# Average pooling over a 537 MB tensor: two loads of a partition from one run of 128 KB, their means in one store run of 32 KB

## The chip, the core and the metric

The kernel runs on one core of a Trainium2 chip. A core has an on-chip memory (SBUF) of 128 partitions, 16 DMA engines that move data between SBUF and the chip's main memory (HBM), and engines with a program each. Three of them matter here: VectorE (DVE) adds, ScalarE (ACT) scales and issues most stores, SyncE (SP) issues the loads. What SP issues goes through one queue (q1 in the profile) and what ACT issues through another (q10); both queues are worked off by the same 16 DMA engines. The metric is the time of one execution on the device in microseconds; less is better.

## The reference

```python
def setup_inputs():
    return {"x": np.random.randn(64, 256, 8192).astype(np.float32),
            "kernel_size": 4, "stride": 4}

def reference(x, kernel_size, stride):
    batch, channels, length = x.shape
    out_len = (length - kernel_size) // stride + 1
    output = np.zeros((batch, channels, out_len), dtype=np.float32)
    for i in range(out_len):
        start = i * stride
        output[:, :, i] = np.mean(x[:, :, start : start + kernel_size], axis=2)
    return output
```

Every four neighbouring numbers of the last axis become their mean. Window and step are equal and divide the row, so the whole tensor can be taken as one flat line of 134,217,728 numbers in groups of four: 536.87 MB are read and 134.22 MB are written, whatever the tiling.

## The kernel before

The flat line is cut into 64 **blocks** of 8.39 MB. A block lies in HBM as 128 rows of 64 KB (`FULL` = 16384 numbers), one row to each partition, one behind the other: partition p of block n has the row n·128 + p. Two input buffers (`xt0`, `xt1`, 64 KB in each partition) hold one block each, even blocks in the first and odd ones in the second. Two output buffers (`ot0`, `ot1`, 32 KB in each partition) hold the means of a **pair** of blocks each, 16 KB for a block.

A block goes through four steps. SP loads it (`load`, line 62, a DMA of 128 rows of 64 KB). DVE adds neighbours in place (line 75, 16384 numbers of a partition become 8192) and adds neighbours again into the output buffer (line 77, 4096 sums). When both blocks of a pair are summed, ACT multiplies the whole output buffer by 1/4 (line 93). Then ACT issues one store of the pair (line 96): 2 × 128 rows of 16 KB, since in HBM the means of one block form a stretch of 2 MB and those of the next block the stretch after it.

```python
xb = x.rearrange("b c l -> (b c l)").rearrange("(n p m) -> n p m", p=P, m=FULL)
ob = out.rearrange("b c l -> (b c l)").rearrange("(n p m) -> p n m", p=P, m=M)
```

The order is written out by hand, with semaphores. `take(engine, sem, n)` (line 59) lets an engine wait until a semaphore has reached n, and takes n off it. DVE waits for `full[k]` (the load of buffer k has landed) and, at the first block of a pair, for `stored[q]` (the store that last read the output buffer has landed). After the second addition DVE raises `free`; SP waits for it and issues the load of the block after the next into the buffer just freed. So while DVE works on one buffer, the load of the other one is in the queue or on its way. ACT waits for `summed`, and its store for the end of its own multiplication (`scaled`).

The loop (line 115) does four blocks a turn, 60 in all. The last four are written out. Blocks 60 and 61 (lines 122 to 139): each is scaled by itself, the first is stored by ACT (line 135), the second by SP (line 139), where its store stands in SP's queue behind the loads of blocks 62 and 63. Block 62 (lines 141 to 148) is scaled by itself and stored by SP. Block 63 comes in two loads of 128 rows of 32 KB (`TAIL`, line 112); each half is summed, scaled (line 156) and stored by ACT (line 158, 128 rows of 8 KB). Last, SP waits for all stores.

Of the kernel before, what the change touches and what calls it, by code (L numbers as in the profile page):

```python
# [1 line left out]

# [4 lines left out]


FULL = 16384
PAIR = 2  # L10
ROUND = 2 * PAIR

TAIL = (8192, 8192)


@with_exitstack
def kernel(
    ctx: ExitStack,
    tc: tile.TileContext,
    x: bass.AP,  # L20
    kernel_size: bass.AP,
    stride: bass.AP,
    out: bass.AP,
):
    nc = tc.nc
    K, S = int(kernel_size), int(stride)
    assert K == S == 4
    B, C, L = x.shape
    assert L % K == 0
    P = nc.NUM_PARTITIONS  # L30
    dt = x.dtype
    add, mult = mybir.AluOpType.add, mybir.AluOpType.mult

    M = FULL // K
    blocks = B * C * L // P // FULL
    loop = blocks - ROUND
    assert blocks * P * FULL == B * C * L and blocks % ROUND == 0 and sum(TAIL) == FULL
    xb = x.rearrange("b c l -> (b c l)").rearrange("(n p m) -> n p m", p=P, m=FULL)
    ob = out.rearrange("b c l -> (b c l)").rearrange("(n p m) -> p n m", p=P, m=M)


    xt0 = ctx.enter_context(nc.sbuf_tensor([P, FULL], dt))
    xt1 = ctx.enter_context(nc.sbuf_tensor([P, FULL], dt))
    ot0 = ctx.enter_context(nc.sbuf_tensor([P, PAIR * M], dt))
    ot1 = ctx.enter_context(nc.sbuf_tensor([P, PAIR * M], dt))
    xt, ot = [xt0, xt1], [ot0, ot1]


    full = [nc.alloc_semaphore(f"full{k}") for k in range(2)]
    piece = [nc.alloc_semaphore(f"piece{k}") for k in range(len(TAIL))]  # L50
    free = nc.alloc_semaphore("free")
    summed = nc.alloc_semaphore("summed")
    summed_last = nc.alloc_semaphore("summed_last")
    scaled = nc.alloc_semaphore("scaled")
    scaled_last = nc.alloc_semaphore("scaled_last")
    stored = [nc.alloc_semaphore(f"stored{k}") for k in range(2)]

    def take(engine, sem, n):
        engine.wait_ge(sem, n).then_inc(sem, -n)  # L59

    def load(i, k):
        d = nc.sync.dma_start(out=xt[k][:, :], in_=xb[i])
        d.then_inc(full[k], 16)
        return d

    for k in range(2):
        tc.no_tile_sem_insts.add(load(k, k).ins.name)
    tc.close()  # L70
    tc.compile()  # L71

    def sums(t, o):
        w = t.shape[1]
        nc.vector.tensor_tensor(out=t[:, : w // 2], in0=t[:, ::2], in1=t[:, 1::2], op=add)  # L75
        nc.vector.drain()
        return nc.vector.tensor_tensor(  # L77
            out=o, in0=t[:, : w // 2 : 2], in1=t[:, 1 : w // 2 : 2], op=add
        )

    def pair(i, q, ahead):

        for k in range(PAIR):
            take(nc.vector, full[k], 16)
            if k == 0:
                take(nc.vector, stored[q], 16)
            sums(xt[k][:, :], ot[q][:, k * M : (k + 1) * M]).then_inc(free, 1)
            take(nc.sync, free, 1)
            if k == 1:
                nc.sync.sem_inc(summed, 1)  # L90
            ahead(k)
        take(nc.scalar, summed, 1)
        nc.scalar.mul(ot[q][:, :], ot[q][:, :], 1.0 / K).then_inc(scaled, 1)  # L93
        take(nc.scalar, scaled, 1)
        o = ot[q][:, :].rearrange("p (n m) -> p n m", n=PAIR)
        nc.scalar.dma_start(out=ob[:, bass.ds(i, PAIR), :], in_=o).then_inc(stored[q], 16)


    zero = nc.const_aps.tensor(0.0, [P, 1], dt)
    nc.scalar.mul(ot[0][:, :1], zero, 1.0).then_inc(stored[0], 16)  # L100
    nc.scalar.sem_inc(stored[1], 16)

    edges = [sum(TAIL[:i]) for i in range(len(TAIL) + 1)]
    pieces = list(zip(edges[:-1], edges[1:]))
    xe, oe = xb[blocks - 1], ob[:, blocks - 1, :]

    def ahead_of_last(k):
        if k == 0:
            load(blocks - 2, 0)
        else:  # L110
            for sem, (a, b) in zip(piece, pieces):
                nc.sync.dma_start(out=xt[1][:, a:b], in_=xe[:, a:b]).then_inc(sem, 16)

    engines = (mybir.EngineType.SP, mybir.EngineType.DVE, mybir.EngineType.Activation)
    with nc.Fori(0, loop // ROUND, 1, engines=engines) as r:
        for q in range(2):
            i = r * ROUND + q * PAIR
            pair(i, q, lambda k: load(i + (PAIR + k), k))

    for k in range(PAIR):
        o = ot[0][:, k * M : (k + 1) * M]
        take(nc.vector, full[k], 16)
        if k == 0:
            take(nc.vector, stored[0], 16)
        sums(xt[k][:, :], o).then_inc(free, 1)
        take(nc.sync, free, 1)
        nc.sync.sem_inc(summed, 1)
        ahead_of_last(k)  # L130
        take(nc.scalar, summed, 1)
        if k == 0:
            nc.scalar.mul(o, o, 1.0 / K).then_inc(scaled, 1)  # L133
            take(nc.scalar, scaled, 1)
            nc.scalar.dma_start(out=ob[:, loop, :], in_=o).then_inc(stored[0], 16)
        else:
            nc.scalar.mul(o, o, 1.0 / K).then_inc(scaled_last, 1)  # L137
            take(nc.sync, scaled_last, 1)
            nc.sync.dma_start(out=ob[:, loop + 1, :], in_=o).then_inc(stored[0], 16)

    take(nc.vector, stored[1], 16)
    take(nc.vector, full[0], 16)
    o = ot[1][:, :M]
    sums(xt[0][:, :], o).then_inc(summed_last, 1)
    take(nc.scalar, summed_last, 1)
    nc.scalar.mul(o, o, 1.0 / K).then_inc(scaled_last, 1)  # L146
    take(nc.sync, scaled_last, 1)
    nc.sync.dma_start(out=ob[:, blocks - 2, :], in_=o).then_inc(stored[1], 16)


    for sem, (a, b) in zip(piece, pieces):
        o = ot[1][:, M + a // K : M + b // K]
        take(nc.vector, sem, 16)
        sums(xt[1][:, a:b], o).then_inc(summed_last, 1)
        take(nc.scalar, summed_last, 1)
        nc.scalar.mul(o, o, 1.0 / K).then_inc(scaled, 1)  # L156
        take(nc.scalar, scaled, 1)
        nc.scalar.dma_start(out=oe[:, a // K : b // K], in_=o).then_inc(stored[1], 16)
    take(nc.sync, stored[0], 32)
    take(nc.sync, stored[1], 16 * (1 + len(TAIL)))  # L160


# [1 line left out]
_INS = ['x', 'kernel_size', 'stride']  # L164
_OUTS = [((64, 256, 2048), 'float32')]

_NUMBERS = {'kernel_size': 4, 'stride': 4}


# [26 lines left out]
```

## Time and profile before

| what | value |
|---|---|
| median of 3 runs | 1553.11 us (1552.67 to 1555.31) |
| profiled execution, its own time | 1553.16 us |
| span of the profiled execution | 1551.8 us |
| DVE busy | 839.9 us (54%) |
| ACT busy | 227.0 us (15%) |
| 16 DMA engines, moved over the span | 671.10 MB, 432 GB/s |
| DMA packets, both queues | 18240 |

The span runs from the first to the last record of the execution; the own time is 1.36 us longer. "Busy" of an engine counts its instructions, not its waiting and not its issuing of DMAs. A DMA engine works its queue off in packets; here a packet is one row of a transfer (64, 32, 16 or 8 KB) or the 4 bytes that raise the semaphore when the engine's share is done. A transfer of 128 rows gives each of the 16 engines 8 rows and one such mark. The trace has a record of each packet, with its start, its duration and its queue; the 18240 packets are 8064 rows of 64 KB, 256 of 32 KB, 8064 of 16 KB, 256 of 8 KB, and 1600 marks.

### The profile page before, as it was taken

Reading aid. Unit: us, or ns where it says so; the run is one execution under the profiler, and the core shown is the slowest. Engines: PE = TensorE matmul, PEld = TensorE weight load, DVE = VectorE, ACT = ScalarE, POOL = GpSimd, SP = SyncE. Lnnn points to the kernel's source line nnn. Section 1 sums busy time; section 2 is a strip of 40 time slices with the busy share of each in tenths; the row PEclk is TensorE's granted clock in tenths of the full one; section 3 lists DMA queues with packets and bytes.
Section 4 is the critical chain, followed back from the end, with each engine's and each line's share of the span. In section 5 each row is a group of like instructions: output and inputs, shape, how many; then the busy total and the mean of one; then the engine's idle time right before and its main releaser. Section 6 shows DMA issues by size and latency. Waiting matters only on the chain. (4 is left out here: it accounts for less than half of the span.)

```text
span 1551.8 us, 942 instructions
## 1 busy us (share of the span) xinstructions
DVE 839.9 (54%) x130; ACT 227.0 (15%) x37; POOL 0.2 (0%) x4
## 2 busy tenths in 40 slices
DVE  3645646456465564654646546455464554645546
ACT  0111011110111101111011110111101111011111
POOL 0000000000000000000000000000000000000000
DMA  9999999999999999999999999999999999999999
GB/s 414 419 444 441 417 439 432 439 441 416 433 432 439 446 434 417 432 433 446 439 436 434 413 440 439 439 432 438 414 439 439 432 439 438 416 437 432 439 432 413
DMA packets 18240, 671.10 MB, mean 432 GB/s; under 512 B 1600, under 2 KB 1600, under 8 KB 1600
## 3 DMA queue, kind: packets, MB, share of 16 engines
q1 hardware_dynamic: 9648, 541.07, 80.5%
q10 hardware_dynamic: 8592, 130.03, 19.6%
HBM read 536.87 MB, written 134.22 MB: 432 GB/s over the span
## 5 line engine op out<-in xcount | busy, mean ns | idle before, releaser
L75 DVE TENSOR_TENSOR xt<-xt 128x8192 f32<-128x8192 f32 (+1 forms) x65 | 556.5, 8561 | 699.4 <-DVEq L59 699.4
L93 ACT ACTIVATE ot<-ot 128x8192 f32<-128x8192 f32 x30 | 210.9, 7029 | 1246.2 <-ACTq L59 1246.2
L77 DVE TENSOR_TENSOR ot<-xt 128x4096 f32<-128x4096 f32 (+1 forms) x65 | 283.4, 4360 | 4.9
L146 ACT ACTIVATE ot<-ot 128x4096 f32<-128x4096 f32 x1 | 3.6, 3616 | 20.6 <-ACTq L59 20.6
L137 ACT ACTIVATE ot<-ot 128x4096 f32<-128x4096 f32 x1 | 3.6, 3616 | 20.3 <-ACTq L59 20.3
L133 ACT ACTIVATE ot<-ot 128x4096 f32<-128x4096 f32 x1 | 3.6, 3616 | 17.4 <-ACTq L59 17.4
L156 ACT ACTIVATE ot<-ot 128x2048 f32<-128x2048 f32 x2 | 3.8, 1909 | 12.1 <-ACTq L59 12.1
L100 ACT ACT_TABLE_LOAD x1 | 1.3, 1283 | 2.4 <-PEq L71 2.4
L100 ACT ACTIVATE ot<-const-float32-0.0 128x1 f32<-128x1 f32 x1 | 0.2, 202 | 0.0
L177 POOL MEMSET const-bfloat16-1.0<- 128x1 bf16 x1 | 0.1, 102 | 0.0
L177 POOL MEMSET const-uint8-127<- 128x1 uint8 x1 | 0.1, 102 | 0.0
L177 POOL MEMSET const-float32-0.0<- 128x1 f32 x1 | 0.1, 99 | 0.2 <-issue 0.2
L177 POOL MEMSET const-float32-1.0<- 128x1 f32 x1 | 0.1, 99 | 0.0
## 6 DMA issues: line engine op xcount, KB each, us to landing
out_dram<-ot ACTq DMA_DIRECT2D x30, 4096.0 KB, 51.7
xt<-in_x_dram SPq DMA_DIRECT2D x2, 4096.0 KB, 29.9
out_dram<-ot SPq DMA_DIRECT2D x2, 2048.0 KB, 27.2
out_dram<-ot ACTq DMA_DIRECT2D x1, 2048.0 KB, 45.3
out_dram<-ot ACTq DMA_DIRECT2D x2, 1024.0 KB, 9.1
xt<-in_x_dram SPq DMA_DIRECT2D x63, 34.7
```

The source lines that it names most:

```text
L75: nc.vector.tensor_tensor(out=t[:, : w // 2], in0=t[:, ::2], in1=t[:, 1::2], op=add)
L77: return nc.vector.tensor_tensor(out=o, in0=t[:, : w // 2 : 2], in1=t[:, 1 : w // 2 : 2], op=add)
L93: nc.scalar.mul(ot[q][:, :], ot[q][:, :], 1.0 / K).then_inc(scaled, 1)
L100: nc.scalar.mul(ot[0][:, :1], zero, 1.0).then_inc(stored[0], 16)
L133: nc.scalar.mul(o, o, 1.0 / K).then_inc(scaled, 1)
L137: nc.scalar.mul(o, o, 1.0 / K).then_inc(scaled_last, 1)
L146: nc.scalar.mul(o, o, 1.0 / K).then_inc(scaled_last, 1)
L156: nc.scalar.mul(o, o, 1.0 / K).then_inc(scaled, 1)
L177: nc = _bacc.Bacc("TRN2", target_bir_lowering=False, num_devices=1)
```

## The change

Blocks are paired in HBM too. A pair now is a **run** of 16.8 MB that lies in HBM as 128 rows of 128 KB, one for each partition. The first load of a run brings the first 64 KB of every such row, the second load the other 64 KB (`xr[n, k]`). So the rows of one load, still 64 KB long, are 128 KB apart instead of 64 KB. The means of a run are 32 KB in a row for each partition (`orun[n]`), and a store of a run is 128 rows of 32 KB. The 32 runs are numbered 0 to 31.

At the end, run 30 (blocks 60 and 61 before) goes through the same function `pair` as the loop's runs: scaled at once by ACT, and stored by SP in one store, which stands in SP's queue behind the loads of run 31. Run 31 has no store of its own for its first block: ACT scales the first block when the first half of the second is summed, scales that half, and stores both together (128 rows of 24 KB); the last half is stored as before (128 rows of 8 KB).

```diff
-    loop = blocks - ROUND
+    runs = blocks // PAIR
-    xb = x.rearrange("b c l -> (b c l)").rearrange("(n p m) -> n p m", p=P, m=FULL)
-    ob = out.rearrange("b c l -> (b c l)").rearrange("(n p m) -> p n m", p=P, m=M)
+    xr = x.rearrange("b c l -> (b c l)").rearrange("(n p k m) -> n k p m", p=P, k=PAIR, m=FULL)
+    orun = out.rearrange("b c l -> (b c l)").rearrange("(n p m) -> n p m", p=P, m=PAIR * M)
...
-    def load(i, k):
-        d = nc.sync.dma_start(out=xt[k][:, :], in_=xb[i])
+    def load(n, k):
+        d = nc.sync.dma_start(out=xt[k][:, :], in_=xr[n, k])
...
-    def pair(i, q, ahead):
+    def pair(n, q, ahead, store):
...
+        done = scaled if store is nc.scalar else scaled_last
         take(nc.scalar, summed, 1)
-        nc.scalar.mul(ot[q][:, :], ot[q][:, :], 1.0 / K).then_inc(scaled, 1)
-        take(nc.scalar, scaled, 1)
-        o = ot[q][:, :].rearrange("p (n m) -> p n m", n=PAIR)
-        nc.scalar.dma_start(out=ob[:, bass.ds(i, PAIR), :], in_=o).then_inc(stored[q], 16)
+        nc.scalar.mul(ot[q][:, :], ot[q][:, :], 1.0 / K).then_inc(done, 1)
+        take(store, done, 1)
+        store.dma_start(out=orun[n], in_=ot[q][:, :]).then_inc(stored[q], 16)
...
-    xe, oe = xb[blocks - 1], ob[:, blocks - 1, :]
+    xe, oe = xr[runs - 1, 1], orun[runs - 1]
...
-            load(blocks - 2, 0)
+            load(runs - 1, 0)
...
-    with nc.Fori(0, loop // ROUND, 1, engines=engines) as r:
+    with nc.Fori(0, (runs - 2) // 2, 1, engines=engines) as r:
         for q in range(2):
-            i = r * ROUND + q * PAIR
-            pair(i, q, lambda k: load(i + (PAIR + k), k))
+            n = r * 2 + q
+            pair(n, q, lambda k: load(n + 1, k), nc.scalar)
+    pair(runs - 2, 0, ahead_of_last, nc.sync)
-    for k in range(PAIR):
-        o = ot[0][:, k * M : (k + 1) * M]
...
-        if k == 0:
-            nc.scalar.mul(o, o, 1.0 / K).then_inc(scaled, 1)
-            take(nc.scalar, scaled, 1)
-            nc.scalar.dma_start(out=ob[:, loop, :], in_=o).then_inc(stored[0], 16)
-        else:
-            nc.scalar.mul(o, o, 1.0 / K).then_inc(scaled_last, 1)
-            take(nc.sync, scaled_last, 1)
-            nc.sync.dma_start(out=ob[:, loop + 1, :], in_=o).then_inc(stored[0], 16)
     take(nc.vector, stored[1], 16)
     take(nc.vector, full[0], 16)
-    o = ot[1][:, :M]
-    sums(xt[0][:, :], o).then_inc(summed_last, 1)
-    take(nc.scalar, summed_last, 1)
-    nc.scalar.mul(o, o, 1.0 / K).then_inc(scaled_last, 1)
-    take(nc.sync, scaled_last, 1)
-    nc.sync.dma_start(out=ob[:, blocks - 2, :], in_=o).then_inc(stored[1], 16)
-    for sem, (a, b) in zip(piece, pieces):
+    sums(xt[0][:, :], ot[1][:, :M]).then_inc(summed_last, 1)
+    for k, (sem, (a, b)) in enumerate(zip(piece, pieces)):
+        take(nc.vector, sem, 16)
+        sums(xt[1][:, a:b], ot[1][:, M + a // K : M + b // K]).then_inc(summed_last, 1)
+        if k == 0:
+            take(nc.scalar, summed_last, 1)
+            nc.scalar.mul(ot[1][:, :M], ot[1][:, :M], 1.0 / K)
         o = ot[1][:, M + a // K : M + b // K]
-        take(nc.vector, sem, 16)
-        sums(xt[1][:, a:b], o).then_inc(summed_last, 1)
         take(nc.scalar, summed_last, 1)
         nc.scalar.mul(o, o, 1.0 / K).then_inc(scaled, 1)
         take(nc.scalar, scaled, 1)
-        nc.scalar.dma_start(out=oe[:, a // K : b // K], in_=o).then_inc(stored[1], 16)
-    take(nc.sync, stored[0], 32)
-    take(nc.sync, stored[1], 16 * (1 + len(TAIL)))
+        c = 0 if k == 0 else M + a // K
+        d = M + b // K
+        nc.scalar.dma_start(out=oe[:, c:d], in_=ot[1][:, c:d]).then_inc(stored[1], 16)
+    take(nc.sync, stored[0], 16)
+    take(nc.sync, stored[1], 16 * len(TAIL))
```

More of the change, by code (lines that the diff above doesn't have):

```diff
@@ L68 @@
     for k in range(2):
-        tc.no_tile_sem_insts.add(load(k, k).ins.name)
+        tc.no_tile_sem_insts.add(load(0, k).ins.name)
     tc.close()
@@ L114 @@
     engines = (mybir.EngineType.SP, mybir.EngineType.DVE, mybir.EngineType.Activation)
-    with nc.Fori(0, loop // ROUND, 1, engines=engines) as r:
+    with nc.Fori(0, (runs - 2) // 2, 1, engines=engines) as r:
         for q in range(2):
-            i = r * ROUND + q * PAIR
-            pair(i, q, lambda k: load(i + (PAIR + k), k))
-    for k in range(PAIR):
-        o = ot[0][:, k * M : (k + 1) * M]
-        take(nc.vector, full[k], 16)
-        if k == 0:
[L126 to L132, printed above, removed]
-            nc.scalar.mul(o, o, 1.0 / K).then_inc(scaled, 1)
-            take(nc.scalar, scaled, 1)
-            nc.scalar.dma_start(out=ob[:, loop, :], in_=o).then_inc(stored[0], 16)
-        else:
-            nc.scalar.mul(o, o, 1.0 / K).then_inc(scaled_last, 1)
-            take(nc.sync, scaled_last, 1)
-            nc.sync.dma_start(out=ob[:, loop + 1, :], in_=o).then_inc(stored[0], 16)
+            n = r * 2 + q
+            pair(n, q, lambda k: load(n + 1, k), nc.scalar)
+    pair(runs - 2, 0, ahead_of_last, nc.sync)
     take(nc.vector, stored[1], 16)
     take(nc.vector, full[0], 16)
-    o = ot[1][:, :M]
-    sums(xt[0][:, :], o).then_inc(summed_last, 1)
-    take(nc.scalar, summed_last, 1)
-    nc.scalar.mul(o, o, 1.0 / K).then_inc(scaled_last, 1)
-    take(nc.sync, scaled_last, 1)
-    nc.sync.dma_start(out=ob[:, blocks - 2, :], in_=o).then_inc(stored[1], 16)
-    for sem, (a, b) in zip(piece, pieces):
+    sums(xt[0][:, :], ot[1][:, :M]).then_inc(summed_last, 1)
[5 more added lines that the diff above has]
+            nc.scalar.mul(ot[1][:, :M], ot[1][:, :M], 1.0 / K)
         o = ot[1][:, M + a // K : M + b // K]
-        take(nc.vector, sem, 16)
-        sums(xt[1][:, a:b], o).then_inc(summed_last, 1)
         take(nc.scalar, summed_last, 1)
```

## The prediction

> **What bounds the kernel now.** I read the page's head, the waits and the DMA parts first, then the stretches with and without stores, the order of time at both ends, and last the records of single DMA packets.
>
> ```profile
> span 1551.8 us, 942 instructions
> DVE 839.9 (54%) x130; ACT 227.0 (15%) x37; POOL 0.2 (0%) x4
> ...
> DMA  9999999999999999999999999999999999999999
> ...
> DMA packets 18240, 671.10 MB, mean 432 GB/s; under 512 B 1600, under 2 KB 1600, under 8 KB 1600
> ...
> q1 hardware_dynamic: 9648, 541.07, 80.5%
> q10 hardware_dynamic: 8592, 130.03, 19.6%
> ```
>
> No engine is near full, while the packets of the two queues take 80.5% and 19.6% of the 16 DMA engines' time: all of it. The waits say the same.
>
> ```profile
> ACT ot L93 <- ACTq L59: 1246.2, 30, 51.8
> DVE xt L75 <- DVEq L59: 699.4, 65, 23.1
> ```
>
> DVE waits 699.4 us for loads and ACT for DVE; both have room. Work of DVE or ACT counts only if a DMA engine runs empty because of it. Two stretches (after their length: busy us of DVE, ACT and POOL, the clock, the DMA engines' busy share, GB/s):
>
> ```profile
> 5.00:60.00 55.00, 26.24 (x4) 4.26 (x1) 0.00 (x0) 1.00 0.99 428
> 80.00:1500.00 1420.00, 771.84 (x118) 207.46 (x30) 0.00 (x0) 1.00 1.00 434
> ```
>
> The first stretch has loads alone, the second loads with stores: the engines are full in both (packets are counted where they end, so a short stretch is rough at its edges).
>
> The packet records give the price of a row on one engine, as the distance of two starts in an unbroken sequence:
>
> ```
> row          64 KB   32 KB   16 KB    8 KB
> ns            2414    1209     607     306
> ```
>
> That is 602 ns for 16 KB, and 4 to 5 ns for each row. Loads take the same alone or beside stores. In the loop each engine alternates strictly: a load row, a store row, 2414 + 607 = 3021 ns. Load to store bytes are 4:1 in these rows and in the work, so the store queue never empties: store 1 is issued at 106.05, store 0's last row ends at about 112. Per engine, 504 × 2414 + 16 × 1209 + 504 × 607 + 16 × 306 + 100 marks × 5 ns = 1547.3 us of rows; the records run from 1.8 to about 1550.9, with gaps of 0.2 us in all. The remaining 1.5 us is slow load rows: 0.68 us at the first rows of the run, 0.10 at 20 to 64 us, **0.67 us where the first store joins the loads, at 64 to 75**, and 0.01 us in the 1425 us after it. So: the time is the number and price of rows, plus whatever leaves an engine without one.
>
> **The change, part by part.** The profiled execution is the base: 1553.16 us, 0.05 above the median of 1553.11.
>
> Store rows: runs 0 to 30 each had 16 rows of 16 KB per engine and now have 8 of 32 KB: 31 × 8 × (2 × 607 − 1209 = 5 ns) = 1.24 us less. In run 31, 16 + 8 KB become 24 KB: 607 + 306 against 306 + 602 = 908, 5 ns × 8 = 0.04. Two transfers fewer save two marks, 0.01. Together **−1.29 us**. A written 32 KB row is not in the trace; the written 8 and 16 KB rows carry on to 306 + 3 × 301 = 1209, and the read row is 1209.
>
> Load rows: same number, same length, 128 KB apart. All 8064 whole rows, at a distance of 64 KB, stand at 2418 ns from the 5th to the 95th percentile, so the memory behind them is not what sets their price: 0. The bounds are 0 and the slowest group in the trace, some 2900 ns (+0.49 us a row, +247 us); I take 0, the row that 16,000 packets share.
>
> Alternation: a store row is now 32 KB, so a store takes 8 × (2414 + 1209) = 29.0 us instead of 48.3, and for 48.3 − 29.0 = 19.3 us of each run loads are alone. Two things follow.
>
> (a) Can loads alone run a queue dry? A load alone takes 8 × 2414 = 19.3 us; in that time the other buffer must be summed and reloaded.
>
> ```profile
> 23.11 8.69 DVE L75 TENSOR_TENSOR xt<-xt 128x8192 f32<-128x8192 f32 x1 [23.11 <-DVEq L59]
> 31.88 4.43 DVE L77 TENSOR_TENSOR ot<-xt 128x4096 f32<-128x4096 f32 x1
> 42.32 8.69 DVE L75 TENSOR_TENSOR xt<-xt 128x8192 f32<-128x8192 f32 x1 [6.01 <-DVEq L59]
> 51.10 4.43 DVE L77 TENSOR_TENSOR ot<-xt 128x4096 f32<-128x4096 f32 x1
> ...
> 61.79 8.69 DVE L75 TENSOR_TENSOR xt<-xt 128x8192 f32<-128x8192 f32 x1 [6.26 <-DVEq L59]
> 63.03 0.44 ACTq L96 DMA_DIRECT2D out_dram<-ot  x1
> ```
>
> The run's own start shows it: loads alone land every 19.3 us; DVE ends at 36.31, SP issues at once (0.33 us), and the previous load's rows last until 41.1: 4.5 us of cover, and no gap in the records. Cost 0.
>
> (b) Stores now join running loads once a run, 30 times instead of once. The one such joining in the loop cost 0.67 us an engine. Bounds: nothing, or that each time. For nothing speak the last loads. Store rows end at 1527; for nine microseconds loads are alone; then ACT's queue, empty since 1527, joins SP's store rows at 1540.4 and costs 0.01 us. And in the first stretch alone each issue of a DMA lengthened the rows in flight on nearly all engines by 10 to 15 ns, while in the late stretch the issue at 1530.30 shows on one engine, by 3 to 8. The engines seem to carry, from their first store on, a cushion that loads alone don't use up. Against it: that joining met stores, not loads. I take it that the first joining pays (for a row twice as long, 1.27 instead of 0.67 if it is the reading of one store row: **+0.6**) and the others nothing. The small hiccups of loads alone (0.10 us in the 44 us before the first store, next to none in the late stretch) would be 1.3 us over 30 × 19.3 us at most: **+0.2**.
>
> The end.
>
> ```profile
> 1530.30 0.34 SPq L148 DMA_DIRECT2D out_dram<-ot  x1
> ...
> 1537.33 4.42 DVE L75 TENSOR_TENSOR xt<-xt 128x4096 f32<-128x4096 f32 x1 [2.78 <-DVEq L59]
> 1541.83 2.29 DVE L77 TENSOR_TENSOR ot<-xt 128x2048 f32<-128x2048 f32 x1
> 1544.24 1.91 ACT L156 ACTIVATE ot<-ot 128x2048 f32<-128x2048 f32 x1 [7.66 <-ACTq L59]
> 1546.26 0.34 ACTq L158 DMA_DIRECT2D out_dram<-ot  x1
> ```
>
> Before, the rows left when the last load is through are 16 × 607 + 16 × 306 ns = 14.6 us (lines 139, 148, 158). Now they are run 30's store, wholly behind the loads in SP's queue, and run 31's: 8 × (1209 + 908 + 306) = 19.4 us. So the last load ends 4.8 us earlier, about 1531. DVE then follows its own pace: block 62 lands at about 1511.5 and is done at 1525.5, each half takes 6.8 us (the first has landed by 1521), so 1532.4 and 1539.2; ACT's 1.91 and the issue give 1541.6. In 1546.26's place that is early: the queues hold rows until about 1550, 2.45 us of them the last store's own, so 5.9 us of other rows cover the 2.1 us that the last store took from its issue to its first row. Cost 0. The removed multiplications (L133, L137, 3.62 each, now one of 7.03) and the moved one (L146) lie on ACT, which waits there 17 to 20 us each time. SP waits for `scaled_last` before run 30's store with nothing behind it but its final waits.
>
> Sum: −1.29 + 0.6 + 0.2 = −0.5, so 1553.16 − 0.5 = **1552.6 us**, no change that a measurement of this kernel can tell (I count 0.2%, 3.1 us, as that).
>
> **The rivals.**
>
> 1. *Every joining costs (slower).* 29 more times 0.67 us: 1552.6 + 19.4 = 1572; with 1.27 us, 1589. For it: the only joining of stores to loads in the trace. Against it: what the late stretch shows. It decides from 0.12 us a joining on (3.6 / 29). Chance 0.25, half of it below 1572.
> 2. *The wider distance slows load rows (slower).* 7 ns on 504 rows is 3.5 us; a row at +1% gives 1565, at +20% (the slow group) 1800. Against it, every row of the loop has the same price now, so the distance of 64 KB leaves room. Chance 0.05. The Trainium skill, "DMA: Bandwidth & Descriptors", section "Latency and other measured facts", says that rows 512 KiB apart moved at 207 GB/s a direction where 214 was full, and far less from 2 MiB on; by its 3.4% on the loads it would be 41 us, 1594, but its distance is four times this one, and no row here shows it.
> 3. *A load queue runs dry in the stretches alone (slower).* Were the 4.5 us of cover short by 1 us, 30 times 1 us: 1583. The start shows the opposite. Chance 0.02.
> 4. *Merged stores save more than their rows (faster).* Row prices can't give it: −1.29 with neither addition is 1551.9; 1550.0 would need 14 ns a pair of rows instead of 5. Chance 0.08, for a price of long written rows that the trace lacks. The Trainium skill, "DMA: Bandwidth & Descriptors", section "Anatomy of one DMA — SWDGE (gpsimd) path", gives about 2 us fixed for each transfer; for two transfers fewer that would be an estimated 4 us, 1549; here transfers follow each other without a gap, and the measurement counts.
>
> **How the numbers follow.** Forecast 0.60, own range 1550.3 to 1555; slower 0.25 + 0.05 + 0.02 = 0.32; faster 0.08. Leaving out the faster tail below 1550 and what lies above 1575 (the dearer joinings, wide distances, about 0.1) gives 1550 to 1575.
>
> **What would show it.** Right: 64 KB rows at 2418 ns, store rows at 1213, stores landing in some 30 us instead of 51.7, DVE's waits uneven (some 6 us after a load alone, more after one beside a store) instead of about 11 throughout, the last store issued near 1541.6, no gaps. Rival 1: load rows longer by about half a microsecond wherever a store begins, once each 48 us. Rival 2: all load rows longer. Rival 3: gaps at load changes. It would be wrong most likely at (b), where two joinings had to stand for thirty.

## The result: 1.0% slower, and the profile after

The changed kernel takes 1569.37 us in the median of 5 executions (1567.69 to 1570.23) against 1553.11: a ratio of 1.0101, 95% interval 1.0086 to 1.0115. It is slower by about 16 us. The forecast was 1552.6 with slower at 0.32. The range (1550 to 1575) holds the time, and rival 1 names the direction and nearly the size.

The page of the changed kernel: span, DMA engines, packets, and for each queue its packets, MB and share of the 16 engines.

```profile
span 1567.4 us, 935 instructions
DVE 839.8 (54%) x130; ACT 226.8 (14%) x36; POOL 0.2 (0%) x4
...
DMA  9999999999999999999999999999999999999998
...
DMA packets 14112, 671.09 MB, mean 428 GB/s; under 512 B 1568, under 2 KB 1568, under 8 KB 1568
...
q1 hardware_dynamic: 9504, 541.07, 80.6%
q10 hardware_dynamic: 4608, 130.03, 19.2%
```

4128 packets fewer, the same bytes, the DMA engines still reported as full, and 15.6 us more. Nothing here says why: a DMA engine that takes longer over a row counts as just as busy (80.6% and 19.2% for the two queues, against 80.5% and 19.6%). The two stretches of before (without stores, and with them) in the changed kernel:

```profile
5.00:60.00 55.00, 26.23 (x4) 4.57 (x1) 0.00 (x0) 1.00 1.00 433
80.00:1500.00 1420.00, 760.85 (x116) 203.84 (x29) 0.00 (x0) 1.00 1.00 430
```

430 instead of 434 GB/s over 1420 us is 0.9%: the loss lies in the loop and not at the ends. The DMA issues (KB each, median us from issue to landing), the waits, and one run of the loop in order of time:

```profile
out_dram<-ot ACTq DMA_DIRECT2D x30, 4096.0 KB, 33.5
...
DVE xt L76 <- DVEq L60: 710.2, 63, 22.8
...
1423.04 7.03 ACT L95 ACTIVATE ot<-ot 128x8192 f32<-128x8192 f32 x1 [41.77 <-ACTq L60]
1423.13 20.93 SPq L63 DMA_DIRECT2D xt<-in_x_dram  x2
1430.29 8.69 DVE L76 TENSOR_TENSOR xt<-xt 128x8192 f32<-128x8192 f32 x1 [7.47 <-DVEq L60]
1430.31 0.34 ACTq L97 DMA_DIRECT2D out_dram<-ot  x1
...
1458.78 8.69 DVE L76 TENSOR_TENSOR xt<-xt 128x8192 f32<-128x8192 f32 x1 [15.30 <-DVEq L60]
```

The same of the kernel before:

```profile
out_dram<-ot ACTq DMA_DIRECT2D x30, 4096.0 KB, 51.7
...
1416.62 8.69 DVE L75 TENSOR_TENSOR xt<-xt 128x8192 f32<-128x8192 f32 x1 [11.20 <-DVEq L59]
...
1440.57 8.69 DVE L75 TENSOR_TENSOR xt<-xt 128x8192 f32<-128x8192 f32 x1 [10.75 <-DVEq L59]
```

A store lands in 33.5 us instead of 51.7, so each run has a stretch of loads alone. DVE waits 7.5 and 15.3 us in turn instead of about 11, as forecast for uneven loads. A store that starts while load rows are running is called a **joining** below. The packet records show where the time is. One DMA engine around a joining at 701 us (start in ns, kind, bytes, duration in ns; a mark is the 4 bytes that raise the semaphore):

```
693270  load   65536  2418
695684  mark       4     9
695690  load   65536  2418
698104  load   65536  3002
701103  store  32768  1213
702313  load   65536  2418
704727  store  32768  1213
```

The load row right ahead of the first store row takes 3002 ns instead of 2418; everything else has its price. Between 80 and 1500 us the slow part of load rows adds up to 12.9 us an engine (29 joinings, **0.44 us each** in the mean; single ones from 0 to 0.9). Of it 8.5 us is in load rows that have a load row before and a store row behind them, 3.2 us in load rows between store rows, nearly all in the first few microseconds of a store, and 1.0 us in the first row of a load. Store rows stand at 1213 ns throughout.

The balance: slow rows 15.1 us an engine instead of 1.5 (+13.6), rows −1.3: the engines' mean end moves by 12.5 us, from 1550.95 to 1563.5 (the remaining 0.2 is gaps). The loss differs by engine, and from about 700 us on two engines run some 4 us behind the others; the last one ends at 1567.1, 3.6 us behind the mean, where before that was 0.5 (+3.1). 12.5 + 3.1 gives the 15.6 us of the span.

### The profile page after: what moved, and what is told of

Its sections match the earlier page's. It is cut to its first block, busy times and chain, and to the rows that moved or that the text cites. A ratio compares the mean times of both kernels' runs of the same rounds, so it can differ in the third digit from the quotient of the medians.

```text
span 1567.4 us, 935 instructions
## 1 busy us (share of the span) xinstructions
DVE 839.8 (54%) x130; ACT 226.8 (14%) x36; POOL 0.2 (0%) x4
## 3 DMA queue, kind: packets, MB, share of 16 engines
q1 hardware_dynamic: 9504, 541.07, 80.6%
q10 hardware_dynamic: 4608, 130.03, 19.2%
## 5 line engine op out<-in xcount | busy, mean ns | idle before, releaser
L95 ACT ACTIVATE ot<-ot 128x8192 f32<-128x8192 f32 x31 | 217.9, 7029 | 1306.3 <-ACTq L60 1306.3
L134 ACT ACTIVATE ot<-ot 128x4096 f32<-128x4096 f32 x1 | 3.6, 3617 | 13.4 <-ACTq L60 13.4
## 6 DMA issues: line engine op xcount, KB each, us to landing
out_dram<-ot ACTq DMA_DIRECT2D x30, 4096.0 KB, 33.5
out_dram<-ot ACTq DMA_DIRECT2D x1, 3072.0 KB, 12.5
```

What stands on the lines that cost most here:

```text
L95: nc.scalar.mul(ot[q][:, :], ot[q][:, :], 1.0 / K).then_inc(done, 1)
L134: nc.scalar.mul(ot[1][:, :M], ot[1][:, :M], 1.0 / K)
```

## Experiments

Every time is a median beside executions of the kernel before on the same chip (1552.9 to 1553.1); where there is no interval, there was one execution. "Slow rows" is the time by which rows exceed their price, for one engine, after the first 80 us. "Rows left" is the time from the end of a load's issue to the end of the load ahead of it on the earliest engine: what the engine still has to do when its next work arrives. Both are from the packet records.

### Which part of the change?

One queue for loads and stores:

```diff
-            pair(n, q, lambda k: load(n + 1, k), nc.scalar)
+            pair(n, q, lambda k: load(n + 1, k), nc.sync)
```

> The changed kernel with every run's store issued by SP, so that loads and stores stand in one queue and no store ever joins running loads from a second queue. Theory J (what costs is the joining: some 0.4 us an engine each time the empty store queue is filled beside running loads): the 64 KB rows go back to 2418 ns throughout and the time is 1553.2 - 1.3 (store rows) = about 1551.5 us, a little under the kernel before. Rival D (rows of a load 128 KB apart cost more): nothing changes, about 1569. Rival T (the turn from reading to writing costs, whichever queue it comes from): it happens as often as in the changed kernel, about 1567 to 1569.

Measured 1556.81 us, ratio 1.0024 (1.0014 to 1.0033). The packets of all loop stores are now q1's:

```profile
span 1555.5 us, 920 instructions
...
q1 hardware_dynamic: 13824, 666.90, 99.2%
q10 hardware_dynamic: 288, 4.19, 0.6%
```

Most of the loss is gone with the second queue, so T (the turn) and D (the distance) fall. Slow rows are 2.1 us, mostly in the last load row ahead of a store, and the last engine ends some 3 us behind the mean; together they are the 5 us that J's number lacks. The turn within a queue isn't free, but costs some 0.05 us a time.

The same addresses in 16 KB rows:

```diff
-        store.dma_start(out=orun[n], in_=ot[q][:, :]).then_inc(stored[q], 16)
+        for h in range(PAIR):
+            c, d = h * M, (h + 1) * M
+            store.dma_start(out=orun[n][:, c:d], in_=ot[q][:, c:d]).then_inc(stored[q], 16)
...
```

> The changed kernel with each run's store of 32 KB rows issued as two stores of 16 KB rows one right behind the other (same addresses, same bytes, loads unchanged). Load and store rows are 64 to 16 KB again, so the store queue should be about as long filled as in the kernel before. Theory J: back to the rows of the kernel before, 1552.5 to 1554 us, store rows landing after some 50 us, 64 KB rows at 2418 ns. Rival D: the loads' distance is unchanged, so about 1569.

Measured 1553.05 us, ratio 1.0000 (0.9990 to 1.0009); slow rows 0.3 us.

```profile
1421.24 8.69 DVE L77 TENSOR_TENSOR xt<-xt 128x8192 f32<-128x8192 f32 x1 [17.02 <-DVEq L61]
...
1439.38 8.69 DVE L77 TENSOR_TENSOR xt<-xt 128x8192 f32<-128x8192 f32 x1 [4.96 <-DVEq L61]
```

DVE waits 17.0 and 5.0 us in turn, more unevenly than in the changed kernel, and rows left are 9.4 and 3.4 us: uneven loads alone cost nothing where the store queue stays filled with 16 KB rows. The loads still lie 128 KB apart: the distance costs nothing (rival 2 falls). The Trainium skill's rule on row pitch ("DMA: Bandwidth & Descriptors", "Latency and other measured facts"; 207 instead of 214 GB/s a direction at 512 KiB) does not begin at 128 KB in this kernel; no run here has 512 KiB.

The layout of before with the rhythm of the changed kernel:

```diff
-        d = nc.sync.dma_start(out=xt[k][:, :], in_=xb[i])
-        d.then_inc(full[k], 16)
+        for c in (0, FULL // 2):
+            d = nc.sync.dma_start(out=xt[k][:, c : c + FULL // 2], in_=xb[i][:, c : c + FULL // 2])
+            d.then_inc(full[k], 16)
...
```

> The kernel before, with each load issued as two loads of 32 KB rows; layout, stores and their 16 KB rows as before. Rows alternate 32 to 16 KB, so a store is through in 16 x (1209 + 607) ns = 29 us and the store queue is empty for 19 us of each run, as in the changed kernel, without any of its layout. Row prices alone: 504 x (2 x 1209 - 2414) = +2.0 us and 64 marks, 0.3 us: 1555.4. Theory J: 30 joinings of 0.4 us more, 1566 to 1571 us. Rival D, and rival W (written rows of 32 KB cost something beside loads): 1555.4.

Measured 1557.53 us, ratio 1.0029 (1.0018 to 1.0040); slow rows 1.0 us. J (each joining costs) fails: 30 stores joined loads after a stretch alone and paid 0.03 us each. Rows and marks gave 1555.4; the rest is 0.8 us of slow rows, 0.4 us of gaps and the last engine. A joining is not dear in itself.

### Which rows?

The loop's stores cut to w numbers of a partition:

```diff
-        store.dma_start(out=orun[n], in_=ot[q][:, :]).then_inc(stored[q], 16)
+        w = 128 if store is nc.scalar else PAIR * M
+        store.dma_start(out=orun[n][:, :w], in_=ot[q][:, :w]).then_inc(stored[q], 16)
```

> The changed kernel with the 30 stores of the loop cut to 128 numbers (512 bytes) of each partition; the rest of these runs is left out of the output. A store joins the loads as often as in the changed kernel but brings next to no bytes. Row prices alone (1236.0 us of load rows, 30 x 8 small rows of an estimated 24 ns, 19.4 us at the end, 5.3 us around): about 1266 us. If a joining costs a fixed start, 0.4 us and the lag of the slowest engine: 1278 to 1285. If it is the time to read the first row of the store: about 1267, and load rows at 2418 ns.

Measured 1266.78 us: a joining has no fixed start that costs.

With w = 4096 and 6144, and then the whole store beside load rows of 32 KB (the edit to `load` as above):

> The changed kernel with the 30 stores of the loop cut to the first 16 KB of each partition (the second half of these runs' means is left out of the output): 64 KB load rows, 16 KB store rows, a store queue that is empty for some 19 us of each run. Row prices from the changed kernel's forecast without any joining, 1551.9 - 30 x 8 x 0.602 = 1407.4 us. Theory R (a joining costs what the reading of the first store row takes beyond a cushion that the engine holds from its first joining on, some 0.6 us, the price of a 16 KB row): load rows before a store at 2418 ns, 1407 to 1410 us. Rival L (a joining costs 0.4 us whenever the load rows are of 64 KB, as in the changed kernel, and nothing where they are of 32 KB): 1419 to 1424 us.

> The same with the loop's stores cut to the first 24 KB of each partition. Row prices 1551.9 - 30 x 8 x 0.301 = 1479.7 us. Theory R: 0.9 us of reading against a cushion of some 0.6 to 0.8, so 0.1 to 0.3 us a joining, 3 to 9 us and a part of the slowest engine's lag: 1483 to 1492 us, between the kernels with 16 and with 32 KB rows. Rival L: 0.4 us a joining and the lag, 1492 to 1496 us.

> The changed kernel with each load issued as two loads of 32 KB rows: store rows of 32 KB join load rows of 32 KB, once a run. Row prices 1551.9 + 2.3 = 1554.2 us. Theory R: the first store row is as long as in the changed kernel, so 0.4 us a joining and the lag, 1566 to 1573 us. Rival L (32 KB load rows take a joining without loss, as they did with 16 KB store rows): 1555 to 1558 us.

Measured 1407.79, 1481.48 and 1557.79 us (the last with a ratio of 1.0030, 1.0017 to 1.0043). Slow rows 0.4, 0.7 and 2.3 us. The second time lies under what either theory expected. L falls with the first, and R with the last, since 32 KB store rows beside 32 KB load rows should have paid 0.4 us a joining and paid less than 0.1. With w = 7168:

> The changed kernel with the loop's stores cut to the first 28 KB of each partition (the last 4 KB of these runs' means are left out of the output). Row prices 1551.9 - 30 x 8 x 0.151 = 1515.7 us. 24 KB rows cost nearly nothing a joining, 32 KB rows 0.42 us. Rival H, with its limit between 88 and 96 KB for both rows: either nothing (1516 to 1518) or about 0.2 us a joining and some lag (1521 to 1528). Theory C: between the two, 1517 to 1523; the cover at the change of loads lies between those of the two kernels.

Measured 1518.51 us, slow rows 2.0 us, 1.7 us of it before 550 us: up to there 0.05 to 0.35 us a joining, then next to nothing. So in these kernels the loss came only with long rows on both sides, 64 KB with 28 to 32 KB. One thing held in all kernels up to here that join from a second queue: the *first* joining costs (0.02 us with 512 byte rows, 0.4 to 0.7 with 16 KB, 0.8 with 24 KB, 0.5 to 1.0 with 28 and 32 KB), and the second doesn't. It looks as if something is built up at the first. In the changed kernel, the third pays again.

### What uses it up?

In the changed kernel, rows left at the issue of a load are 13.0 and 5.6 us in turn ahead of the third joining, and shrink to 7.2 and 1.7 us late in the run, as two engines fall behind. In the kernel before they are 9.0 to 9.2 us throughout the loop. The first experiment has half of the additions, so that loads are issued earlier:

```diff
-        nc.vector.tensor_tensor(out=t[:, : w // 2], in0=t[:, ::2], in1=t[:, 1::2], op=add)
-        nc.vector.drain()
-        return nc.vector.tensor_tensor(
-            out=o, in0=t[:, : w // 2 : 2], in1=t[:, 1 : w // 2 : 2], op=add
-        )
+        return nc.vector.tensor_tensor(out=o, in0=t[:, ::4], in1=t[:, 1::4], op=add)
```

> The changed kernel with one addition for each block in place of two (only the first two of every four numbers are summed, so half of the sum is left out). Loads, stores, their rows and the multiplications stay; DVE takes some 4.4 us a block instead of 13.1, so SP issues each load some 8.7 us earlier, and the rows still in the queue at the issue of a load rise from about 2 to 5 us to 10 us and more. Theory C (the read-ahead that one joining builds up is used up at the change of loads, because the next load comes late into the queue): no loss at joinings but the first, 1552 to 1554 us. Rival H (a 64 KB load row and a 32 KB store row together are more than an engine can hold ahead): the losses stay, 1564 to 1570 us.

Measured 1553.32 us, ratio 1.0010 (0.9994 to 1.0027), at least 9.5 us of rows left, slow rows 0.9 us. The rows are those of the changed kernel, so H (too much for an engine to hold) falls. The place of the joining has moved too: it is at the change of loads or 2.4 us (one row) behind it. (One of its ten executions took 1565.4 us.) The opposite, with 16 KB store rows and a useless addition:

```diff
+        nc.vector.tensor_tensor(
+            out=t[:, w // 2 : 5 * w // 8], in0=t[:, : w // 4 : 2], in1=t[:, 1 : w // 4 : 2], op=add
+        )
+        nc.vector.drain()
```

> The kernel with 16 KB store rows cut out of the changed one (1407.8 us), with one more, useless addition of 128x2048 in DVE for each block, 2.3 us: SP issues each load that much later, and the rows left in the queue at the issue fall from 4.8 us to about 2.5. Theory C: joinings begin to cost, 0.2 to 0.5 us each, 1414 to 1425 us with the lag. Rival H: the rows are the same, 1408 to 1410 us.

Measured 1408.86 us with 2.5 us of rows left, slow rows 0.5 us. C's number fails: a late issue alone does next to nothing where store rows are short.

More cover had also moved the place in a load at which the store joins. Two runs part these: the delay given back in ACT, and the changed kernel with a shorter scaling.

```diff
# on the kernel with more cover
+        nc.scalar.mul(ot[q][:, :], ot[q][:, :], 1.0)
+        nc.scalar.drain()
+        nc.scalar.mul(ot[q][:, :2048], ot[q][:, :2048], 1.0)
+        nc.scalar.drain()
         nc.scalar.mul(ot[q][:, :], ot[q][:, :], 1.0 / K).then_inc(done, 1)
# on the changed kernel
-        nc.scalar.mul(ot[q][:, :], ot[q][:, :], 1.0 / K).then_inc(done, 1)
+        w = 1024 if store is nc.scalar else PAIR * M
+        nc.scalar.mul(ot[q][:, :w], ot[q][:, :w], 1.0 / K).then_inc(done, 1)
```

> The kernel with one addition a block (more cover at the change of loads; half of the sum is left out) with two useless multiplications by 1 in ACT before the scaling of a run, 7.0 + 1.9 us: the store joins the loads some 9 us later, at about the place in a load where it joins in the changed kernel, while the loads stay issued early. Theory C (the cover at the change of loads decides): 1552 to 1556 us, as without the delay. Rival P (the place in a load at which the store joins decides): the losses come back, 1564 to 1570 us.

> The changed kernel with ACT scaling only the first 1024 of 8192 sums of a partition in the loop's runs (the rest is stored unscaled): DVE and the issue of loads stay as they are, and the store joins some 6 us earlier. Theory C: cover as in the changed kernel, so the losses stay, 1564 to 1571 us. Rival P: the place in the load is moved and the losses go, 1552 to 1556 us.

Measured 1553.09 us, ratio 0.9999 (0.9990 to 1.0009), and 1553.72 us, ratio 1.0005 (0.9995 to 1.0015). The first speaks for C: joining 7.2 us behind a load's start, a place inside the changed kernel's range (4.8 to 12 us, 28% of its joinings at 6.9 to 7.9), with 12 us of rows left, no loss. The second speaks against C as put: rows left 3.7 us and no loss. There the store rows join at the change of loads itself, 0 to 2.4 us behind it, where they also joined with more cover. Two more, on the changed kernel: each block scaled when it is summed, and the two useless multiplications as above:

```diff
...
-        take(nc.scalar, summed, 1)
-        nc.scalar.mul(ot[q][:, :], ot[q][:, :], 1.0 / K).then_inc(done, 1)
-        take(store, done, 1)
+        for k in range(PAIR):
+            o = ot[q][:, k * M : (k + 1) * M]
+            take(nc.scalar, summed, 1)
+            nc.scalar.mul(o, o, 1.0 / K).then_inc(done, 1)
+        take(store, done, PAIR)
```

> The changed kernel with ACT scaling each block of a run as soon as it is summed (two multiplications of 3.6 us instead of one of 7.0 after the second block). The result is complete; the store joins the loads 3.4 us earlier, and the loads are issued as in the changed kernel, with some 5 us of rows left in the queue. Theory C2 (the load is issued too late for the engine's read-ahead, which goes on undisturbed if store rows stand in the queue by then, and else is shortened and built up again at the next joining): the store now comes into the queue before the rows of the old load end, so most of the losses go, 1552 to 1556 us. Rival P (losses belong to a joining two to four rows behind the change of loads): the joining is one row earlier, about half of them stay, 1558 to 1564 us.

> The changed kernel with two useless multiplications by 1 in ACT before each scaling (8.9 us), so that the store joins at about the seventh row of a load instead of the third to fourth; loads are issued as in the changed kernel. Theory C2: the read-ahead lost at the change of loads does not come back by itself, so the losses stay, 1564 to 1571 us. Rival P: away from the third and fourth row there is no loss, 1552 to 1556 us. Rival C3 (loads alone rebuild the read-ahead in some 10 us): 1552 to 1556 us too.

Measured 1580.95 us, ratio 1.0182 (1.0159 to 1.0205), and 1553.10 us, ratio 1.0001 (0.9992 to 1.0010). Both miss C2. Storing earlier made it **worse**, and storing 8.9 us *later* took the whole loss away. The page and the order of time of the late joining:

```profile
span 1551.7 us, 929 instructions
...
80.00:1500.00 1420.00, 771.79 (x118) 463.09 (x87) 0.00 (x0) 1.00 1.00 434
...
1405.95 0.33 SPq L63 DMA_DIRECT2D xt<-in_x_dram  x1
...
1416.26 8.69 DVE L76 TENSOR_TENSOR xt<-xt 128x8192 f32<-128x8192 f32 x1 [10.62 <-DVEq L60]
1422.21 0.34 ACTq L101 DMA_DIRECT2D out_dram<-ot  x1
...
1440.67 8.69 DVE L76 TENSOR_TENSOR xt<-xt 128x8192 f32<-128x8192 f32 x1 [11.22 <-DVEq L60]
```

DVE waits 10.6 and 11.2 us, evenly. The store now lies half in one load and half in the next, so both take about 24 us and none 19; the rows left are 8 to 9 us at nearly all issues (7.6 at least), as in the kernel before. The expectation was wrong to hold the rows left at 5 us: *where the store joins decides how the loads' times are parted, and so how late the next load comes*. In the kernel with blocks scaled one by one they fall to 3.0 us at once and 1.3 later, and slow rows are 25.5 us. There the second joining already paid 0.7 us, with 5.2 us left (in the changed kernel 6.9, and it was free), so that the second is free is no rule. The third paid next to nothing, with 3.0 us left. The last run holds the late place and takes the time away:

```diff
+        for d in (4, 8):
+            h, g = w // 2, w // d
+            nc.vector.tensor_tensor(out=t[:, h : h + g], in0=t[:, : 2 * g : 2], in1=t[:, 1 : 2 * g : 2], op=add)
+            nc.vector.drain()
         return nc.vector.tensor_tensor(
...
+        nc.scalar.mul(ot[q][:, :2048], ot[q][:, :2048], 1.0)
+        nc.scalar.drain()
         nc.scalar.mul(ot[q][:, :], ot[q][:, :], 1.0 / K).then_inc(done, 1)
```

> The kernel with the late joining, its delay moved from ACT to DVE: two useless additions a block (4.4 and 2.3 us) ahead of the second one, and only 1.9 us of the useless multiplication left. The store joins at about the same row of a load as with the late joining, but each load is issued 6.7 us later, with some 2 us of rows left in the queue instead of 8.5. Theory C (how late the load is issued decides, wherever the store joins): the losses come back, 1562 us and more. Rival P (the third and fourth row behind a change of loads decide): no losses, 1552 to 1556 us.

Measured 1606.67 us, ratio 1.0339 (1.0322 to 1.0356). The store joins behind the fifth row, 10 to 14 us after a load's start, with −0.6 to 4 us of rows left. The losses are back, some 20 us of them in the rows ahead of a joining (0.7 us a time), so P (the place decides) falls. Here queues also ran dry, with gaps of some 20 us an engine and 9.9 us of slow first rows of loads, so the total is not the price of the joinings alone.

The kernels with 64 KB load rows side by side (rows left at the tighter issue, after the second joining and late):

```
store row   rows left us        joins behind change   slow rows us   time us
32 KB       5.6, later 1.7      4.8 to 12 us          13.3           1569.4
32 KB       3.0, later 1.3      2.4 to 9 us           25.5           1581.0
32 KB       about 2 or less     10 to 14 us           35.4           1606.7
32 KB       8 to 9              12 us                 0.4            1553.1
32 KB       12                  7.2 us                0.4            1553.1
32 KB       9.5 to 11.5         0 to 2.4 us           0.9            1553.3
32 KB       4.2, later 3.7      0 to 2.4 us           1.2            1553.7
28 KB       5.4, later 3.3      4.8 to 7.3 us         2.0            1518.5
24 KB       5.5, later 3.9      4.8 to 7.2 us         0.7            1481.5
16 KB       2.5                 7.2 to 9.7 us         0.5            1408.9
```

## Why the prediction was wrong

**The step that failed is (b)**, "the others nothing": 29 joinings were put at 0 and cost 12.9 us an engine, and 3.1 us more because the engines no longer end together, a term the sum didn't have. Its upper end, 0.67 us each, gave 1572; 0.44 us and the lag gave 1569. The evidence against it was real but too narrow: a joining that met store rows of 16 KB at the end of the run. Of the two small terms, the first joining took 1.02 us instead of 0.67 (+0.35, where +0.6 was forecast), and rows of loads alone lost 0.1 us (0.2).

That the stated range holds the time, and that rival 1's 1572 came near it, is in part luck. Rival 1's rule, 0.67 us at every joining, doesn't hold either: the second was free, the others cost up to 0.9 us, and with other rows or an earlier issue of the loads they cost next to nothing. Two slips in the working move nothing: 1550.0 us would need about 13 ns a pair of rows in rival 4, not 14, and the price of a load row stood on 8064 packets, not 16,000. The fixed time for each transfer that rival 4 weighed, from a section on another way of issuing DMAs, doesn't show: 30 more stores in the kernel with 16 KB rows took 1553.05 us.

**Step (a) failed with it.** "4.5 us of cover, and no gap in the records. Cost 0." Up to 690 us there is indeed no gap; from then on, with under 2 us of rows left, there are about ten of 0.05 to 0.48 us on all 16 engines together, nearly all at a change of loads, 0.14 us an engine. The criterion was wrong: with 32 KB store rows, losses come with 5.6 us of rows left already. What a late load takes shows at the next joining and in the length of a row, hardly as a gap. Shown: with the rows of the changed kernel, more time left removes the loss (1553.3, 1553.1), wherever the store joins; less time brings it back even at a late joining (1606.7), and makes it larger at an early one (1581.0). Shown too: short store rows don't need that time (0.5 us of slow rows with 2.5 us left).

That the engine reads ahead, that a late load shortens its lead, and that a long store row needs the lead again, is only argued. It fits that the first joining always pays, 0.4 to 1.0 us from 16 KB rows on, while the second is free with 6.9 us left and pays with 5.2. Against it stand three things that are not settled: a joining at the change of loads goes free with 3.7 us left, the kernel with 28 KB rows stopped paying after 550 us although less was left than before, and with blocks scaled one by one the third joining went free with 3.0 us left, between others that paid. So the time left is a cause, but not the only condition; the place of the joining and the length of its rows count with it.

**What held:** the prices of the rows (written rows of 32 and 24 KB are recorded with 1213 and 912 ns, and 4 ns less from start to start, 1209 and 908, as worked out); load rows unchanged by the distance; stores landing in some 30 us (33.5); DVE's uneven waits. The end held as well: the last store was issued at 1557.01 us, that is 15.4 us behind the forecast 1541.6, so the end adds nothing to the 15.6 us of the span. The saving of 1.29 us is in the rows, and no kernel made it visible in its time: with the loss removed, the changed kernel computes everything in 1553.10 us (ratio 1.0001 to before). Fixing it only brings it level; no version found here beats the kernel before.

## What to carry to other kernels

Where the DMA engines are the bound, "no gap" and "100% busy" don't clear a change: compare the duration of rows of one size, above all ahead of the first row from another queue. A store that is through sooner leaves loads alone for a stretch, and these land faster. The time to free and reissue a buffer, long enough at the mean rate, is then too short; work it out at the fastest load, and ask for more than just no gap. A rhythm in which load and store rows stand in the ratio of their bytes kept both queues filled here (1553.05 us in the changed layout), and was worth more than halving the number of store rows.

## What the runs showed of the hardware

A row's time on a DMA engine was 2414, 1209, 607 and 306 ns for 64, 32, 16 and 8 KB, the same to a nanosecond alone or mixed, and for 32 KB read or written, apart from the slow rows: joining two rows into one buys 4 to 5 ns. Useless work can be a gain: 8.9 us of multiplications by 1 in each run took 16 us off the changed kernel, because its stores then joined the loads at another place. And a loss on some engines seems to feed itself: from about 700 us on, two of 16 engines ran some 4 us behind. A load lands with its last engine, so the others had that much less left when their next load came: 1.7 us instead of 5.6, and the joinings cost 0.6 us in the mean from there on, against 0.3 before.
